# Mixture-of-experts pairs with the fuller expert first, and an arm for pairs of two small experts

## The chip, the cores and the metric

The kernel runs on one core of a Trainium2 chip. The core has five engines with queues of their own: TensorE (PE: matrix products, with a separate row for its weight loads), VectorE (DVE), ScalarE (ACT), GpSimd (POOL) and SyncE (SP), which here issues the loads. Sixteen DMA engines move data between the memory and the core's on-chip buffers. Products are summed in PSUM, a second on-chip memory, and copied out by ACT and DVE. The metric is the time of one execution on the device, in microseconds.

## The reference

Two transformer blocks of two layers each, over 256 tokens of width 1024, in float32. The change lies in the second block, in the mixture of experts that ends each of its two layers. A router picks two of sixteen experts for each token, and an expert is a SwiGLU network of inner width 512:

```python
for e in range(N_EXPERTS):
    he = jax.nn.silu(t @ w_gate[e]) * (t @ w_up[e])
    y = y + combine[:, e:e + 1] * (he @ w_down[e])
```

The router has four groups of four experts, takes the best group for a token, and in it the two best experts. With 256 tokens and two choices an expert has 32 tokens on average. On the inputs that are timed the reference's router gives these counts (expert p and expert p + 8, which the kernel treats as a pair):

| pair | 0 | 1 | 2 | 3 | 4 | 5 | 6 | 7 |
|---|---|---|---|---|---|---|---|---|
| layer 0 | 52, 29 | 24, 50 | 16, 20 | 50, 55 | 9, 48 | 29, 33 | 26, 18 | 32, 21 |
| layer 1 | 12, 79 | 12, 81 | 28, 72 | 22, 78 | 21, 17 | 25, 8 | 20, 14 | 14, 9 |

## The kernel before

All weights are read from memory once, over SP's queue. Most of the program multiplies dense matrices, split into a high and a low part. The expert stage is the function `moe(l, ...)`, called once a layer, and it works on plain float32.

**Pairs and slots.** Experts p and p + 8 share a pair of 128 slots. Each gets 64, or, where one has more than 64 tokens and the other at most 32, 96 and 32 (`ga`, L1757 and L1758). `slot` (L1774) says which slot a token has in a pair, and `onehot(p)` (L1780) makes a 0/1 matrix of it, tokens by slots. `gather` multiplies the normalized tokens with it into `xg_b` (L1828), `places` makes the slots' weights and the transposed matrix for the way back. Tokens that don't fit go to extra rounds behind the eight pairs; on these inputs there are none.

**One pair.** `pair()` computes the gate product (tile pg), the up product (pu), the activation, a transposition (tr), two halves of the down product (pd), and the way back to tokens (py). Gate and up have 8 steps over the width (KD), each half of down has 4. The slots are the stationary side and the weights the moving side, 512 columns wide. Every step issues one product for each strip of columns in `SEG` (L1848): two of 64, or four of 32; strips of different columns work side by side. One such product is two records in the profile.

**Branches.** Which strips a pair needs is known only after routing. `products()` (L1852) puts three arms into TensorE's program and picks one by a register that is read from `gi` (L1760; `reg`, L1931): 64 + 64 for value 2, 96 + 32 for 3, 32 + 96 otherwise. `reg(0)` stands ahead of the first gather in TensorE's queue.

**The ring of weights.** A pair has 12 pieces of 1 MiB: gate, up and down, each in two halves of the contracted width, each for two experts. `pieces()` (L1607) issues the loads in this order into a ring of 20 buffers (RING); a buffer is loaded again when the product that reads it is done. From piece 84 on (the last pair) each load is cut in two. Each load also waits for the load eight places ahead of it. The ring is full by the end of the router; only pair 0's gate frees the first buffers.

**Order.** The order of the engines' instructions follows the program's code, moved by a scheduler where nothing pins it; `pin()` holds the products of a pair in place. In a pair, the next pair's `gather` stands between the up product and the transposition, and again behind the transposition. In the last pair there is none, and the way back of the first half stands between the two parts of the second down half.

Of the kernel before, what the change touches and what calls it, by code (L numbers as in the profile page):

```python
# [7 lines left out]
F32 = mybir.dt.float32  # L8
F32R = mybir.dt.float32r
I32 = mybir.dt.int32  # L10
# [18 lines left out]
RING = 20  # L29
LNEXP = "natural_log_exp_and_others"  # L30
# [95 lines left out]
def build(tc, I, out, dump=None, upto=99):  # L126
    nc = tc.nc
    coff, ctot = _const_layout()
    with ExitStack() as ctx:
# [1456 lines left out]
        def moe(l, a, op, pre=None, post=None):  # L1586


            with ExitStack() as c1:
# [16 lines left out]

                def pieces(upto):  # L1607
# [138 lines left out]

                A2 = [128, 2, 8]
# [11 lines left out]
                gi = mp.tile([128, 8], I32, name="gi")  # L1759
                V.tensor_scalar(gi, ga[:, 0], 0.03125, None, op0=OP.mult)  # L1760
# [8 lines left out]
                V.tensor_scalar(sl[:, :, 0:8], pos[:, :, 0:8], 1.0, None, op0=OP.add)  # L1769
                V.scalar_tensor_tensor(sl[:, :, 8:16], pos[:, :, 8:16], 1.0, ga[:, 0:1, :].to_broadcast(A2),  # L1770
# [15 lines left out]
                ohs = {0: onehot(0)}  # L1786

# [64 lines left out]
                def products(p, x, n_k, w_, gr_, ks=None):  # L1852


                    def arm(n):
                        for k in ks or range(n_k):
                            ws, kp = w_(k)
                            for o, m, e in SEG[n]:
                                mm(p[o:o + m, :], x[:, k, o:o + m], ws[e][kp], start=k == 0, stop=k == n_k - 1,  # L1859
                                   skip_group_check=True)  # L1860
                    if gr_ is None:
                        arm(2)
                        return
                    with tc.issue_after(last[ENG.PE]):
                        with tc.If(gr_ == 2) as c:
                            arm(2)
                        with c.Else():
                            with tc.If(gr_ == 3) as c2:
                                arm(3)
                            with c2.Else():  # L1870
                                arm(1)

                def pair(pl, w_, gr_, nxt=lambda i: None, last_=False):

                    pg, pu = psum("pg"), psum("pu")
                    products(pg, xg_b, KD, lambda k: (w_("exp_w_gate_2", k // 4), k % 4), gr_)
                    products(pu, xg_b, KD, lambda k: (w_("exp_w_up_2", k // 4), k % 4), gr_)
                    act = tm()
                    S.activation(act, pg, AF.Silu)
                    V.tensor_mul(act, act, pu)  # L1880
# [4 lines left out]
                    for i in range(4):  # L1885
                        pin(PE.transpose(p[:, i * 128:(i + 1) * 128], act.rearrange("s (j k) -> s k j", k=4)[:, i], ident))
# [4 lines left out]
                    def down(dd, between=None):  # L1891
                        pd = psum("pd")
                        cs = slice(dd * 512, (dd + 1) * 512)
                        for ks in (range(0, 2), range(2, 4)) if between else (None,):
                            products(pd, hT, 4, lambda k: (w_("exp_w_down_2", k // 2), k % 2 * 2 + dd), gr_, ks)
# [34 lines left out]
                def reg(p):  # L1930
                    return nc.values_load(gi[0:1, p:p + 1], engines=[ENG.PE], min_val=1, max_val=3)  # L1931
# [5 lines left out]
                for p in range(8):  # L1937
# [15 lines left out]
                    pair(pl[p], lambda nm, hf: [wpiece[p, e, nm, hf] for e in range(2)], regs[p], nxt, p == 7)  # L1953
# [7 lines left out]
                with tc.For_i(0, n_extra, 1) as it:  # L1961
# [50 lines left out]
                    pair(places(oh2, w2_, 0), w_, None, last_=True)  # L2012
# [51 lines left out]
```

## Time and profile before

| | |
|---|---|
| median of three runs (lowest, highest) | 2056.05 us (2055.13, 2057.55) |
| the profiled execution, its own time | 2052.47 us |
| its span | 2050.7 us |
| TensorE busy, share of the span | 95% |
| weight loads of TensorE | 78% |
| DVE, ACT | 63%, 36% |
| read from memory over the span | 530.65 MB, 259 GB/s |
| expert stage of layer 0, first gate product to last product | 1411.8 to 1639.5 us |
| expert stage of layer 1, first gate product to end of span | 1807.5 to 2050.7 us |

The shares are means over stages with different limits. Positions are microseconds from the start of the span. A busy TensorE is not a TensorE at its peak, since products are pipelined; the granted clock (PEclk) stands beside it as a share of full speed.

### The profile page before, as it was taken

How to read it: one execution, taken by the hardware profiler on the slowest of the kernel's cores; microseconds unless marked ns; L12 is line 12 of the kernel's file. 1: busy time of each engine (PE TensorE's matmuls, PEld its weight loads, DVE VectorE, ACT ScalarE, POOL GpSimd, SP SyncE). 2: the span in 40 equal slices, each digit the busy share in tenths (PEclk: the TensorE clock that was granted, in tenths of full speed). 3: DMA queues.
4: the chain of work that ended last, by engine and by line, in shares of the span. 5: the costliest groups of instructions: out<-in, count | busy, mean ns of one | idle time of the engine just before them, and what ended most of it. 6: DMA issues, size and time to landing. Idle time of an engine off the chain costs nothing. (4 is left out here: it accounts for less than half of the span.)

```text
span 2050.7 us, 34453 instructions
## 1 busy us (share of the span) xinstructions
PE 1945.3 (95%) x14344; PEld 1599.1 (78%) x14344; DVE 1286.9 (63%) x2188; ACT 734.0 (36%) x1075; POOL 64.6 (3%) x60
## 2 busy tenths in 40 slices
PE   6999999999899999999999999998999889889997
PEld 5889899888699989999999999975444488744443
DVE  6357677858797959796798777853223287533222
ACT  4322222245454444445654445441000167500001
POOL 0000000011010010001010010000000010000000
PEclk8999999999999999999999999999999999989999
DMA  8678697734396869776486946468999544879992
GB/s 296 241 252 297 245 325 270 258 103 124 104 335 216 301 172 321 254 261 236 165 299 210 317 150 218 156 233 327 412 416 413 216 149 145 339 321 416 416 411 90
DMA packets 240525, 534.76 MB, mean 261 GB/s; under 512 B 13132, under 2 KB 168128, under 8 KB 206528
## 3 DMA queue, kind: packets, MB, share of 16 engines
q1 hardware_dynamic: 237424, 531.54, 72.0%
q8 instruction: 162, 2.65, 0.5%
q10 hardware_dynamic: 2896, 0.21, 0.2%
q14 instruction: 43, 0.35, 0.0%
HBM read 530.65 MB, written 1.07 MB: 259 GB/s over the span
## 5 line engine op out<-in xcount | busy, mean ns | idle before, releaser
L448 PE MATMUL pa<-hh,whl 128*128 128x258 f32 (+1 forms) x880 | 252.4, 287 | 3.6 <-ACT hh L516 3.6
L450 PE MATMUL pa<-hh,whl 128*128 128x258 f32 (+1 forms) x880 | 249.5, 283 | 4.9 <-DVE whl L419 4.9
L449 PE MATMUL pa<-hl,whl 128*128 128x258 f32 (+1 forms) x880 | 249.4, 283 | 3.3 <-DVE hl L517 3.3
L448 PE MATMUL pb<-hh,whl 128*128 128x258 f32 (+1 forms) x880 | 249.3, 283 | 0.8 <-ACT s L564 0.8
L449 PE MATMUL pb<-hl,whl 128*128 128x258 f32 (+1 forms) x880 | 249.0, 283 | 0.0
L450 PE MATMUL pb<-hh,whl 128*128 128x258 f32 (+1 forms) x880 | 248.9, 283 | 0.0
L324 DVE SCALAR_TENSOR_TENSOR macc<-modw,cst,macc 128x1024 f32<-128x1024 f32 (+1 forms) x182 | 219.9, 1235 | 23.0 <-DMA modw<-in_w_mod_dram 16.1
L418 ACT ACTIVATE whl<-w13r 128x2048 fp32r<-128x2048 f32 x88 | 168.5, 1914 | 179.7 <-PE pb L450 86.3
L419 DVE TENSOR_TENSOR whl<-w13r,whl 128x2048 fp32r<-128x2048 f32 x88 | 201.6, 2291 | 38.5 <-ACT whl L418 38.5
L450 PE MATMUL py<-gh,whl 128*128 128x256 f32 (+1 forms) x704 | 216.7, 308 | 2.7 <-DVE whl L419 2.7
L448 PE MATMUL py<-gh,whl 128*128 128x256 f32 (+1 forms) x704 | 218.4, 310 | 0.1
L449 PE MATMUL py<-gl,whl 128*128 128x256 f32 (+1 forms) x704 | 216.3, 307 | 0.0
L448 PE MATMUL lin<-hh,whl 128*128 128x258 f32 x640 | 188.6, 296 | 5.6 <-ACT hh L516 5.6
L449 PE MATMUL lin<-hl,whl 128*128 128x258 f32 x640 | 181.9, 285 | 3.3 <-DVE hl L517 3.3
L450 PE MATMUL lin<-hh,whl 128*128 128x258 f32 x640 | 181.4, 284 | 0.0
L448 PEld LDWEIGHTS pa<-hh,whl 128*128 128x128 f32 x880 | 166.8, 189 | 11.6 <-ACT hh L516 3.8
L450 PEld LDWEIGHTS pa<-hh,whl 128*128 128x128 f32 x880 | 167.3, 190 | 5.7 <-DVE whl L419 5.3
L449 PEld LDWEIGHTS pa<-hl,whl 128*128 128x128 f32 x880 | 167.7, 191 | 4.1 <-DVE hl L517 3.9
L448 PEld LDWEIGHTS pb<-hh,whl 128*128 128x128 f32 x880 | 166.8, 190 | 1.8 <-ACT s L564 1.0
L450 PEld LDWEIGHTS pb<-hh,whl 128*128 128x128 f32 x880 | 166.9, 190 | 0.4 <-issue 0.4
L449 PEld LDWEIGHTS pb<-hl,whl 128*128 128x128 f32 x880 | 166.9, 190 | 0.0
L418 ACT ACTIVATE whl<-w2r 128x768 fp32r<-128x768 f32 (+3 forms) x80 | 90.7, 1143 | 160.4 <-PE py L450 106.2
(444 smaller groups left out, 3766.7 us busy)
## 6 DMA issues: line engine op xcount, KB each, us to landing
w13r<-in_ffn_w_dram SPq DMA_DIRECT2D x86, 1024.0 KB
modw<-in_w_mod_dram SPq DMA_DIRECT2D x62, 1024.0 KB
ew<-in_exp_w_down_dram SPq DMA_DIRECT2D x54, 1024.0 KB
ew<-in_exp_w_gate_dram SPq DMA_DIRECT2D x54, 1024.0 KB
ew<-in_exp_w_up_dram SPq DMA_DIRECT2D x52, 1024.0 KB
modw<-in_ada_w_dram SPq DMA_DIRECT2D x48, 1024.0 KB
w2r<-in_ffn_w_dram SPq DMA_DIRECT2D x18, 1536.0 KB
w2r<-in_ffn_w_dram SPq DMA_DIRECT2D x12, 1280.0 KB
```

The source lines that it names most:

```text
L324: V.scalar_tensor_tensor(acc[h], x, c, acc[h], op0=OP.mult, op1=OP.add)
L418: S.activation(h, src, AF.Copy)
L419: V.tensor_sub(l, src, h.bitcast(F32))
L448: mm(p, ah, bh, start=start, stop=False)
L449: mm(p, ah, bl, start=False, stop=False)
L450: mm(p, al, bh, start=False, stop=stop)
```

## The change

For the first two pairs nothing changes but the layout of the activation in `pair()`. From the third pair on (SORTED = 2):

- The expert with more tokens comes first. `swp` says where the two change places, and the loads take the expert's number from a register on SP (`order(p)`), read from rows 1 and 2 of a larger `gi`.
- The branch has three other arms: both experts at most 32 tokens (`light`, value 4), 64 + 64 (value 2), and 96 + 32. In the new arm each expert has 32 slots, and these stand twice, in columns 0 to 63 and 64 to 127. One step multiplies four strips of 32: both experts with a piece of the first half of the contracted width and both with one of the second half. That takes half the steps and leaves two partial sums.
- The partial sums of the gate are added ahead of the activation (`oth`). Those of the up product are added by a product with the identity plus, in a light pair, a matrix that swaps halves (`summing`); it stands in the place of the transposition. Those of down are added by the way back, whose one-hot has the slots twice.
- The same instructions for `oth` and `summing` run in all pairs from the third on, with a factor of 0 where the pair isn't light.
- The router has more small steps on DVE, and `gi` is computed behind the first one-hot.

```diff
+                def order(p):
+                    if p not in orders:
+                        orders[p] = [nc.values_load(gi[0:1, 1 + i, p:p + 1], engines=[ENG.SP], min_val=0, max_val=15)
+                                     for i in range(2)]
+                    return orders[p]
...
-                                wpiece[todo[n + j]] = piece(bufs[(n + j) % RING], I[nm][l, p + 8 * e], nm, hf, ks)
+                                w = I[nm][l, p + 8 * e] if p < SORTED else \
+                                    I[nm][l][bass.ds(order(p)[e], 1)].rearrange("o a b -> (o a) b")
+                                wpiece[todo[n + j]] = piece(bufs[(n + j) % RING], w, nm, hf, ks)
...
-                gi = mp.tile([128, 8], I32, name="gi")
-                V.tensor_scalar(gi, ga[:, 0], 0.03125, None, op0=OP.mult)
+                V.tensor_mul(light, c32[:, 0], c32[:, 1])
+                V.memset(light[:, :SORTED], 0.0)
...
+                V.tensor_tensor(swp[:, SORTED:], swp[:, SORTED:], cnt[:, 1, SORTED:], op=OP.is_lt)
...
+                    V.scalar_tensor_tensor(gl[:, i], light, -32.0, ga[:, i], op0=OP.mult, op1=OP.add)
+                V.tensor_mul(st[:, 0], gl[:, 1], swp)
+                V.tensor_mul(st[:, 1], gl[:, 0], swp)
+                V.tensor_sub(st[:, 1], gl[:, 0], st[:, 1])
...
-                    V.tensor_tensor(oh, iota1[:, None, :].to_broadcast([128, 2, 128]),
-                                    slot[:, :, p:p + 1].to_broadcast([128, 2, 128]), op=OP.is_equal)
+                    V.tensor_tensor(oh[:, :, 0:64], iota1[:, None, 0:64].to_broadcast([128, 2, 64]),
+                                    slot[:, :, p:p + 1].to_broadcast([128, 2, 64]), op=OP.is_equal)
+                    V.scalar_tensor_tensor(oh[:, :, 64:128], iota1[:, None, 64:128].to_broadcast([128, 2, 64]),
+                                           l64[:, p:p + 1], slot[:, :, p:p + 1].to_broadcast([128, 2, 64]),
+                                           op0=OP.subtract, op1=OP.is_equal)
...
+                    def arm_light():
+                        for k in range(h) if ks is None else range(ks[0] // 2, ks[-1] // 2 + 1):
+                            for o in range(4):
+                                ws, kp = w_(k + o // 2 * h)
+                                mm(p[o * 32:o * 32 + 32, :], x[:, k + o // 2 * h, o * 32:o * 32 + 32], ws[o % 2][kp],
+                                   start=k == 0, stop=k == h - 1, skip_group_check=True)
...
+                    a, b, c_ = ((4, arm_light), (2, lambda: arm(2)), lambda: arm(3)) if srt else \
+                        ((2, lambda: arm(2)), (3, lambda: arm(3)), lambda: arm(1))
...
+                    V.scalar_tensor_tensor(x.rearrange("p (h j) -> p h j", h=2), i2[:, ::-1, :], light[:, p:p + 1], i2,
+                                           op0=OP.mult, op1=OP.add)
...
+                        S.activation(oth[0:64, :], pg[64:128, :], AF.Copy, scale=lt[64:128, :])
+                        V.tensor_scalar(oth[64:128, :], pg[0:64, :], lt[0:64, :], None, op0=OP.mult)
+                        V.tensor_add(oth, oth, pg)
+                        S.activation(kj, by_k(oth), AF.Silu)
...
-                        pin(PE.transpose(p[:, i * 128:(i + 1) * 128], act.rearrange("s (j k) -> s k j", k=4)[:, i], ident))
+                        o_ = p[:, i * 128:(i + 1) * 128]
+                        pin(PE.transpose(o_, kj[:, i], ident) if lt is None else mm(o_, kj[:, i], sm_, start=True, stop=True))
```

How instructions move, at three places. First DVE in the router of layer 0, before, from the register's source `gi` to the first one-hot `oh` (a row is a line of the kernel, an operation, what it writes and reads, and the shape):

```order
L1760 TENSOR_SCALAR gi<-ga 128x8
L1770 SCALAR_TENSOR_TENSOR sl<-pos,ga 128x2x8
L1766 TENSOR_TENSOR fit<-pos,ga 128x32
L1804 TENSOR_TENSOR left<-pos,ga 128x16
L1767 TENSOR_TENSOR fit<-fit,ch 128x32
L1805 TENSOR_TENSOR left<-left 128x8
L1772 TENSOR_TENSOR sl<-sl,fit 128x32
L1806 TENSOR_SCALAR left<-left 128x8
L1774 TENSOR_TENSOR slot<-sl 128x16
L1808 SCALAR_TENSOR_TENSOR left<-left 128x8
L1783 TENSOR_TENSOR oh<-c_iota_13207,slot 128x256
```

And the same place of the kernel after, from the first one-hot on:

```order
L1804 TENSOR_TENSOR slot<-sl 128x16
L1849 TENSOR_TENSOR left<-pos,ga 128x16
L1814 TENSOR_TENSOR oh<-c_iota_13207,slot 128x2x64
L1816 SCALAR_TENSOR_TENSOR oh<-c_iota_13207,l_15042,slot 128x2x64
L1827 TENSOR_TENSOR gf<-gf,l_15042 128x8
L1850 TENSOR_TENSOR left<-left 128x8
L1933 SCALAR_TENSOR_TENSOR w_14713<-c_ident,light 128x128
L1828 TENSOR_SCALAR gi<-gf 128x8
```

`gi` stood ten rows ahead of the one-hot; now it stands behind both halves of it, with three rows between, one of them a 128x128 matrix of `summing`.

Second, TensorE, the gate product of pair 3, before (the three arms, each closed by a jump; a row of products counts the instructions of one arm):

```order
L1865 COMPARE_AND_BRANCH
L1859 MATMUL pg<-ew,nx 64x512 x16
L1865 UNCONDITIONAL_BRANCH
L1868 COMPARE_AND_BRANCH
L1859 MATMUL pg<-ew,nx 32x512 x32
L1868 UNCONDITIONAL_BRANCH
L1859 MATMUL pg<-ew,nx 32x512 x32
L1868 UNCONDITIONAL_BRANCH
```

And after:

```order
L1921 COMPARE_AND_BRANCH
L1913 MATMUL pg<-ew,nx 32x512 x16
L1921 UNCONDITIONAL_BRANCH
L1924 COMPARE_AND_BRANCH
L1906 MATMUL pg<-ew,nx 64x512 x16
L1924 UNCONDITIONAL_BRANCH
L1906 MATMUL pg<-ew,nx 32x512 x32
L1924 UNCONDITIONAL_BRANCH
```

The first arm has 16 products of 32 columns; the 64 + 64 arm is now the second and is reached by a second comparison; the arm for 32 + 96 is gone.

Third, SP's queue where the loads of pair 2 begin, before:

```order
L1623 DMA ew<-in_exp_w_down_dram 128x2048 x2
L1623 DMA ew<-in_exp_w_gate_dram 128x2048 x2
L1865 UNCONDITIONAL_BRANCH x2
L1623 DMA ew<-in_exp_w_gate_dram 128x2048 x2
L1623 DMA ew<-in_exp_w_up_dram 128x2048 x2
```

And after:

```order
L1636 DMA ew<-in_exp_w_down_dram 128x2048 x2
L1614 TENSOR_LOAD gi
L1614 ISA x2
L1614 TENSOR_LOAD gi
L1614 ISA x2
L1636 ISA
L1636 DMA ew<-in_exp_w_gate_dram 128x2048
L1921 UNCONDITIONAL_BRANCH x2
L1636 ISA
L1636 DMA ew<-in_exp_w_gate_dram 128x2048
```

Two register loads from `gi` stand ahead of the pair's first load, and one register instruction ahead of each load; before, the same loads were issued back to back.

## Rows read from the trace of the kernel before

**Rows 1.** The page's second part: rate of all transfers in 40 equal slices.

```profile
GB/s 296 241 252 297 245 325 270 258 103 124 104 335 216 301 172 321 254 261 236 165 299 210 317 150 218 156 233 327 412 416 413 216 149 145 339 321 416 416 411 90
```

**Rows 2.** Table by windows, one stretch: stretch, us, engines, PEclk, DMA share, GB/s.

```profile
1441.00:1472.00 31.00, 31.00 (x172) 14.53 (x170) 9.81 (x22) 1.97 (x3) 0.00 (x0) 1.00 1.02 415
```

**Rows 3.** Groups by shape, 1380 to 2051: gate products, count, busy us, mean ns, idle.

```profile
L1859 PE MATMUL pg<-ew,nx 128*64 128x512 f32 x384 | 85.0, 595 | 0.0
...
L1859 PE MATMUL pg<-ew,nx 128*32 128x512 f32 x256 | 28.9, 593 | 1.0 <-issue 0.9
```

**Rows 4.** Timeline of TensorE, pair 2 of layer 0: start us, us, instruction, count.

```profile
1467.92 7.09 PE L1859 MATMUL pg<-ew,nx 128*64 128x512 f32 x32
1474.83 7.04 PE L1859 MATMUL pu<-ew,nx 128*64 128x512 f32 x32
...
1483.69 0.64 PE L1886 MATMUL tr<-c_ident,tm 128*128 128x128 f32 x4
...
1486.05 7.09 PE L1859 MATMUL pd<-ew,tm 128*64 128x512 f32 x32
...
1495.82 7.09 PE L1859 MATMUL pg<-ew,nx 128*64 128x512 f32 x32
```

**Rows 5.** Timeline of TensorE, layer 1, pairs 0, 1 and 3; in brackets the idle before.

```profile
1807.50 7.07 PE L1859 MATMUL pg<-ew,nx 128*32 128x512 f32 x64
...
1837.09 7.07 PE L1859 MATMUL pg<-ew,nx 128*32 128x512 f32 x63 [0.85 <-issue]
...
1903.95 7.05 PE L1859 MATMUL pu<-ew,nx 128*32 128x512 f32 x48 [2.27 <-issue]
```

**Rows 6.** Table by windows: start and end of the refills, and one clock.

```profile
1416.00:1418.00 2.00, 2.00 (x12) 0.69 (x10) 0.00 (x0) 0.00 (x0) 0.00 (x0) 1.00 0.75 184
...
1612.00:1614.00 2.00, 2.00 (x12) 0.63 (x10) 1.33 (x4) 0.00 (x0) 0.00 (x0) 1.00 0.54 210
1616.00:1618.00 2.00, 1.97 (x10) 0.43 (x6) 0.00 (x0) 0.00 (x0) 0.00 (x0) 1.00 0.22 69
...
1814.00:1816.00 2.00, 2.00 (x24) 0.72 (x20) 0.00 (x0) 0.60 (x1) 0.00 (x0) 1.00 0.74 217
...
2010.00:2012.00 2.00, 2.00 (x19) 2.00 (x18) 1.38 (x3) 0.59 (x1) 0.00 (x0) 1.00 0.16 64
...
1904.00:1906.00 2.00, 2.00 (x12) 0.54 (x16) 0.00 (x0) 0.00 (x0) 0.00 (x0) 0.53 1.01 418
```

**Rows 7.** Timeline of TensorE, the last pair of layer 0 and of layer 1.

```profile
1610.88 7.09 PE L1859 MATMUL pg<-ew,nx 128*64 128x512 f32 x32
...
1628.40 5.37 PE L1859 MATMUL pd<-ew,tm 128*64 128x512 f32 x24 [0.83 <-issue]
...
1638.41 1.10 PE L1906 MATMUL py<-dd 128*128 128x256 f32 x7 [0.40 <-DVE dd L1899]
...
2028.85 5.37 PE L1859 MATMUL pd<-ew,tm 128*64 128x512 f32 x24 [0.83 <-issue]
```

**Rows 8.** Timeline of all engines, router of layer 0.

```profile
1403.01 0.17 DVE L1749 TENSOR_SCALAR c<-pos 128x16 f32<-128x16 f32 x1 [0.80 <-PE pos L1743]
...
1403.89 0.16 DVE L1760 TENSOR_SCALAR gi<-ga 128x8 int32<-128x8 f32 x1
...
1404.92 0.42 DVE L1783 TENSOR_TENSOR oh<-c_iota,slot 128x256 f32<-128x256 f32 x1
...
1405.89 5.39 PE L1828 MATMUL ga<-oh,nx 128*128 128x128 f32 x32 [2.93 <-DVE w L1810]
```

**Rows 9.** Timeline of all engines, pair 2 of layer 0: the two evictions.

```profile
1489.80 0.69 ACT L1898 ACTIVATE dd<-pd,sw 128x512 fp32r<-128x512 f32 x1 [14.12 <-PE pd L1859]
1490.52 0.75 DVE L1899 SCALAR_TENSOR_TENSOR dd<-pd,sw,dd 128x512 fp32r<-128x512 f32 x1 [3.67 <-ACT dd L1898]
```

**Rows 10.** Timeline of SP's queue: one issue of a quarter of a piece.

```profile
1508.79 0.33 SPq L1620 DMA_DIRECT2D ew<-in_exp_w_down_dram  x1
```

More of the change, by code (lines that the diff above doesn't have):

```diff
@@ L29 @@
 RING = 20
+SORTED = 2
 LNEXP = "natural_log_exp_and_others"
@@ L1758, in moe @@
                 V.tensor_scalar(ga[:, 1], ga[:, 0], -1.0, 128.0, op0=OP.mult, op1=OP.add)
-                gi = mp.tile([128, 8], I32, name="gi")
-                V.tensor_scalar(gi, ga[:, 0], 0.03125, None, op0=OP.mult)
+                light = mp.tile([128, 8], F32, name="light")
+                V.tensor_mul(light, c32[:, 0], c32[:, 1])
+                V.memset(light[:, :SORTED], 0.0)
+                swp = mp.tile([128, 8], F32, name="swp")
+                V.memset(swp[:, :SORTED], 0.0)
+                V.tensor_copy(swp[:, SORTED:], cnt[:, 0, SORTED:])
+                V.tensor_tensor(swp[:, SORTED:], swp[:, SORTED:], cnt[:, 1, SORTED:], op=OP.is_lt)
+                gl = mp.tile(A2, F32, name="gl")
+                st = mp.tile(A2, F32, name="st0")
+                for i in range(2):
+                    V.scalar_tensor_tensor(gl[:, i], light, -32.0, ga[:, i], op0=OP.mult, op1=OP.add)
+                V.tensor_mul(st[:, 0], gl[:, 1], swp)
+                V.tensor_mul(st[:, 1], gl[:, 0], swp)
+                V.tensor_sub(st[:, 1], gl[:, 0], st[:, 1])
+                l64 = mp.tile([128, 8], F32, name="l64")
+                V.tensor_scalar(l64, light, 64.0, None, op0=OP.mult)
                 pos = mp.tile(E2, F32, name="pos")
@@ L1850, in moe, with products @@
                        1: ((0, 32, 0), (32, 32, 1), (64, 32, 1), (96, 32, 1))}
-                def products(p, x, n_k, w_, gr_, ks=None):
+                def products(p, x, n_k, w_, gr_, srt=False, ks=None):
+                    h = n_k // 2
                     def arm(n):
@@ L1863, in products @@
                         return
+                    a, b, c_ = ((4, arm_light), (2, lambda: arm(2)), lambda: arm(3)) if srt else \
+                        ((2, lambda: arm(2)), (3, lambda: arm(3)), lambda: arm(1))
                     with tc.issue_after(last[ENG.PE]):
-                        with tc.If(gr_ == 2) as c:
-                            arm(2)
+                        with tc.If(gr_ == a[0]) as c:
+                            a[1]()
                         with c.Else():
-                            with tc.If(gr_ == 3) as c2:
-                                arm(3)
+                            with tc.If(gr_ == b[0]) as c2:
+                                b[1]()
@@ L1870, in products, with summing @@
                             with c2.Else():
-                                arm(1)
-                def pair(pl, w_, gr_, nxt=lambda i: None, last_=False):
+                                c_()
+                def summing(p):
+                    x = (w0, w1)[p % 2]
+                    i2 = ident.rearrange("p (h j) -> p h j", h=2)
+                    V.scalar_tensor_tensor(x.rearrange("p (h j) -> p h j", h=2), i2[:, ::-1, :], light[:, p:p + 1], i2,
+                                           op0=OP.mult, op1=OP.add)
+                    return x
@@ L1875, in pair @@
+                def pair(pl, w_, gr_, lt, sm_, srt=False, nxt=lambda i: None, last_=False):
                     pg, pu = psum("pg"), psum("pu")
-                    products(pg, xg_b, KD, lambda k: (w_("exp_w_gate_2", k // 4), k % 4), gr_)
-                    products(pu, xg_b, KD, lambda k: (w_("exp_w_up_2", k // 4), k % 4), gr_)
                     act = tm()
-                    S.activation(act, pg, AF.Silu)
-                    V.tensor_mul(act, act, pu)
+                    kj = act.rearrange("s (k j) -> s k j", k=4)
+                    by_k = lambda x: x.rearrange("s (j k) -> s k j", k=4)
+                    products(pg, xg_b, KD, lambda k: (w_("exp_w_gate_2", k // 4), k % 4), gr_, srt)
+                    if lt is None:
+                        S.activation(kj, by_k(pg), AF.Silu)
+                    else:
+                        oth = tm()
+                        S.activation(oth[0:64, :], pg[64:128, :], AF.Copy, scale=lt[64:128, :])
+                        V.tensor_scalar(oth[64:128, :], pg[0:64, :], lt[0:64, :], None, op0=OP.mult)
+                        V.tensor_add(oth, oth, pg)
+                        S.activation(kj, by_k(oth), AF.Silu)
+                    products(pu, xg_b, KD, lambda k: (w_("exp_w_up_2", k // 4), k % 4), gr_, srt)
+                    V.tensor_mul(kj, kj, by_k(pu))
@@ L1952, in moe @@
                         ohs[p + 1] = onehot(p + 1)
-                    pair(pl[p], lambda nm, hf: [wpiece[p, e, nm, hf] for e in range(2)], regs[p], nxt, p == 7)
+                    pair(pl[p], lambda nm, hf: [wpiece[p, e, nm, hf] for e in range(2)], regs[p],
+                         *((light[:, p:p + 1], summing(p), True) if p >= SORTED else (None, ident, False)), nxt, p == 7)
                     pieces(12 * p + 12 + RING)
@@ L2011, in w_ @@
                         return got[nm, hf]
-                    pair(places(oh2, w2_, 0), w_, None, last_=True)
+                    pair(places(oh2, w2_, 0), w_, None, None, ident, last_=True)
         op = even(mods["a0"])
```

18 lines of the change are left out of this document (14 added, 4 removed).

## The prediction

> **What bounds the kernel now.** I read the slices of the span first: the rate row stands near 412 GB/s in two blocks of slices, 28 to 30 and 34 to 38 [rows 1]. These are the two expert stages; no other stretch stays at such a rate. A table by windows then shows what limits them: 415 GB/s with a DMA share of 1.02, so all sixteen DMA engines are full, and at the same time TensorE is busy for the whole 31 us [rows 2]. Two resources are nearly level, and the question is which of them ends last.
>
> The groups by shape say which arms ran. The gate product has 384 records on 64-column arms, 32 a pair, so 12 pairs; and 256 on 32-column arms, 64 a pair, so 4 pairs [rows 3]. That fits the counts in the section on the reference: no pair but the first four of layer 1 has a count over 64. By the same counts seven pairs from the third on have both experts at 32 tokens or fewer: pairs 2, 6, 7 of layer 0 and 4, 5, 6, 7 of layer 1. They are what I call light.
>
> The timeline of TensorE prices a pair: gate 7.09 us, up 7.04, down 7.09, and the next pair's gate 27.9 us after this one's [rows 4]. The memory needs 12 pieces of 1,048,576 bytes for it; at 415 GB/s a piece takes 2.53 us, a pair 30.3 us. TensorE is the faster of the two, and lives on the lead of 20 pieces in the ring. So I compare two lines. TensorE: pair 7 of layer 0 starts at 1610.9, its down product at 1628.4, and its last product ends at 1639.5 [rows 7]. Memory: the first refill moves at about 1416.8 in layer 0 and 1815 in layer 1; 76 pieces at 2.53 us are 192 us, so an even stream would end at 1608.8 and 2007 [rows 6]. Really the engines finish unevenly: at 1612 to 1614 the share is 0.54 (with a first megabyte for the next stage among it) and 0.22 at 1616 to 1618; in layer 1 0.16 at 2010 to 2012 [rows 6]. I take 1613 and 2010 for the landing of the last piece, with 1608.8 to 1617 and 2007 to 2012 as bounds. Today that is 15 to 19 us before the down product wants it: TensorE sets the end, by this margin and no more.
>
> **The change part by part.**
>
> *Light arms.* Four products of 32 columns side by side cost what two of 64 do: 64 records in 7.07 us [rows 5] against 32 in 7.09 [rows 4]. A light arm has 4 steps in place of 8 for gate and for up, and 4 in place of 8 for the two down halves together, so it halves 7.09 + 7.04 + 7.09: 10.6 us less per light pair, 74 us over seven. Most of this can't reach the end, because the last piece can't land sooner.
>
> *Does pair 7 then wait for memory?* Layer 0: two light pairs before it take 21.2 us off 1610.9; the transposition that becomes a product costs at most a second 0.64 us [rows 4] in each of five pairs, 3 us; the later start below adds 2. Pair 7 is then ready at about 1595, its down product some 10 us after it (3.5 + 3.5 + 3 for activation and transposition), at 1605. The last piece lands at 1613 + 2. TensorE waits some 10 us. In layer 1 three light pairs come before, and it waits longer. So in both layers the end becomes landing plus what is left to do.
>
> *What is left after landing.* Layer 0 needs 11.1 us from the start of down to the end of the last product [rows 7]. The light down takes 3.55 off. The eviction of the first down half, 0.69 on ACT and 0.75 on DVE [rows 9], stood behind 1.8 us of products and now stands behind 0.9, which gives 0.9 back: 8.5 us. Layer 1 has 2050.7 - 2028.85 = 21.9 us from there to the end of the span, so 19.2.
>
> *The clock after a wait.* After an idle of 2.27 us TensorE's granted clock was 0.53, close to the lower level of 1.2 GHz, and 48 records took 7.05 us, where three quarters of 7.07 are 5.3 [rows 5, 6]: 1.8 us lost. I add 1.8 in each layer for the restart in pair 7; bounds 0 (the clock stays up) and 3.5 (all that TensorE still has to do, some 6 us, at half rate for most of it).
>
> *Router.* Ahead of the first one-hot DVE has 28 short instructions where it had 20. Twenty took 1403.01 to 1404.92, 0.096 each [rows 8], so 0.8 us more. The branch register moves behind the one-hot: it is loaded on TensorE's queue ahead of the gather, and gi now comes at about 1406.6, against 1404.05. From gi to the gather it was 1.84 us [rows 8]. If that load is what the gather waited for, it starts at 1408.4, 2.5 us later; if the one-hot was, 0.8. I take 2. Behind the gather stand the first gate product and, through the ring, all refills, so it moves the landing too. The memory hides nothing of it: the ring is full there.
>
> *Gate eviction.* From pair 2 on it is four passes (ACT copy, DVE scale, DVE add, ACT activation) where it was one: 0.69 + 0.75 + 0.75 + 0.69 = 2.9 us by the nearest rows [rows 9]. The up product, 3.5 us in a light arm, hides it. Without that cover, the gather between up and transposition has another microsecond; I cost it at nothing, below 1 us a pair otherwise, and that again only ahead of a wait for memory.
>
> *Loads by register.* SP gets two register loads per pair from pair 2 on and one register instruction ahead of each load. No row shows a load with a register address. The nearest is a plain issue, 0.33 us [rows 10]; SP may take 2.53 us per piece before the stream notices, and up to eight loads are in flight. I take nothing; the other end is the rival below. It can't gain: the engines are full.
>
> *Branches.* A 64 + 64 pair from pair 2 on tests twice, as the 96 + 32 pairs of layer 1 do now, whose gate takes 7.07 us [rows 5]: nothing.
>
> **Sum.** Layer 0: 1613 + 2 + 8.5 + 1.8 = 1625.3 against 1639.5, 14.2 us less. Layer 1 (its span positions as they are now): 2010 + 2 + 19.2 + 1.8 = 2033 against 2050.7, 17.7 less. Together 32. The profiled execution took 2052.5 us, 1.8 more than its span, so 2020.6; the median shown is 3.6 us above that execution, so 2024. Best ends: 1608.8 + 0.8 + 8.5 and 2007 + 0.8 + 19.2, 45 us less, 2011. Worst: 1617 + 2.5 + 8.5 + 3.5 and 2012 + 2.5 + 19.2 + 3.5, 21.5 less, 2034.5.
>
> The Trainium skill (DMA: Bandwidth & Descriptors, Specifications) puts the fabric's ceiling at 435 GB/s and the memory's limit per core at about 358. By the first the 76 pieces would end 9 us sooner in each layer, an estimate of 50 us less; by the second 31 us later, which would leave no gain at all. The trace holds 415 for tens of microseconds, so neither is used above.
>
> **Rivals.**
>
> A. *TensorE keeps waiting for its own instructions.* Six times in these stages it stood still with nothing to wait for ("issue"), for 0.85 to 2.27 us, the shortest and the longest of the six [rows 5]. If each of the four groups of products in a light pair paid 1.75, as they jump over two other arms in half the time, a light pair would lose 7 of 10.6. Pair 7 of layer 0 would be at its down product at 1605 + 14 + 5 = 1624 and end at 1632.5 (7 less), layer 1 at 2028.9 - 31.8 - 7 + 5 = 1995, with 3 x 7 + 5 for the waits 2021, and end at 2040 (11 less): 2038. Against: layer 1's pairs jump now too, and show three of these waits in 16 groups. The Trainium skill (Runtime: NRT & Kernel Launch, Instruction fetch mechanics) says that a taken branch to a place outside the fetched window stalls the engine until it is fetched; by it A is the outcome, and the waits of this trace could be such fetches, though far from one per jump.
>
> B. *TensorE alone sets the time*: 74 less, minus 4 for the router and 6 for the products that replace transpositions, 64: 1992. For it speaks that TensorE is busy throughout [rows 2]; against it that the engines are full in the same row.
>
> C. *The light arms bring nothing*: not entered, or four streams that slow each other. Then only the router's 4 us are left, 2060. The counts and rows 5 speak against it.
>
> D, the other side. *Register addresses make the queue slower than the stream.* Layer 0 and 1 load 144 pieces so. Once SP and the address work take over 2.53 us a piece, each 0.1 us costs 14 us; at 2.75 the gain of 32 is gone, and at 3.0 it is 68 - 32 = 36 slower: 2092. For it: no row shows such a load. Against it: 0.33 us for an issue, a sevenfold reserve.
>
> **Chances.** The forecast 0.71 (2011 to 2035), A 0.13, B 0.05, C 0.04, D 0.07. The prediction is 2024. For 8 in 10 the range takes in half of A and the slack at the fast end: 2009 to 2040. What a measurement of this kernel can tell from no change is 0.2%, 4 us. Faster: forecast, A and B, 0.89. C lies on the border: 0.03 for no change, and 0.08 with D for slower.
>
> **What would show it.** In the profile after: pg groups with 16 steps' records in 3.5 us in seven pairs; waits of TensorE for a DMA of ew, about 10 us in pair 7 of each layer and next to none before; 415 GB/s unchanged; the last product of the expert stage near 1625; a clock near 0.5 just behind the wait; the first gather 2 us later. It is wrong if TensorE is late at pair 7 with "issue" ahead of its groups (A), if the rate falls under 400 in the steady part (D), or if the landing is not the last to come.

## The result, and the profile after

Beside each other on one chip, four runs of either kernel: before 2056.8 us (2055.13 to 2062.48), after 2024.66 us (2020.24 to 2029.16); ratio 0.9839, interval 0.9806 to 0.9872. The change takes 32 us off, and 2024 had been forecast. The profiled execution after took 2027.96 us with a span of 2026.2, one of the longer ones.

The first look goes to the rate in the slices of the page, as in [rows 1].

```profile
GB/s 295 233 252 305 236 320 282 285 76 156 46 349 201 345 134 336 220 328 186 205 233 280 251 216 239 106 208 291 384 415 416 398 139 167 264 276 388 418 415 260
```

Both blocks near 415 GB/s are still there: counted from 0, slices 28 to 31 hold 384 to 416 and slices 36 to 38 hold 388 to 418, and the last slice has 260 where it had 90. The rate has not risen: the same bytes fill the same engines, so what was saved lies elsewhere.

A light pair is the next thing to see: TensorE's timeline, pair 2 of layer 0 (start us, us, instruction, count, in brackets the idle before), against [rows 4].

```profile
1473.06 3.64 PE L1913 MATMUL pg<-ew,nx 128*32 128x512 f32 x32
1476.52 3.62 PE L1913 MATMUL pu<-ew,nx 128*32 128x512 f32 x32
1481.10 2.02 PE L1873 MATMUL ga<-oh,nx 128*128 128x128 f32 x16 [0.96 <-DVE tm L1955]
1482.96 1.06 PE L1962 MATMUL tr<-w,tm 128*128 128x128 f32 x8
...
1485.73 3.64 PE L1913 MATMUL pd<-ew,tm 128*32 128x512 f32 x32
...
1492.88 1.51 PE L1906 MATMUL pg<-ew,nx 128*64 128x512 f32 x6 [0.74 <-PE py L1982]
```

Gate, up and down take 3.6 us where they took 7.1; from this pair's gate to the next it is 19.8 us where it was 27.9. So 8.1 of the 10.6 us arrive. Two small prices stand in the brackets: 0.96 us ahead of the next pair's gather, which waits for the product with up (L1955), and 0.74 ahead of the next gate product.

Where the time goes then is told by pair 7. TensorE's timeline, layer 0, after, against [rows 7]:

```profile
1599.03 3.64 PE L1913 MATMUL pg<-ew,nx 128*32 128x512 f32 x32
1603.46 1.05 PE L1913 MATMUL pu<-ew,nx 128*32 128x512 f32 x4 [0.79 <-PE pg L1913]
1605.36 1.04 PE L1913 MATMUL pu<-ew,nx 128*32 128x512 f32 x2 [0.85 <-DMA ew<-in_exp_w_up_dram]
...
1609.17 1.90 PE L1913 MATMUL pu<-ew,nx 128*32 128x512 f32 x10 [0.22 <-DMA ew<-in_exp_w_up_dram]
...
1613.91 1.05 PE L1913 MATMUL pd<-ew,tm 128*32 128x512 f32 x4 [0.83 <-issue]
1616.03 5.75 PE L1913 MATMUL pd<-ew,tm 128*32 128x512 f32 x20 [1.07 <-DMA ew<-in_exp_w_down_dram]
...
1626.18 1.09 PE L1982 MATMUL py<-dd 128*128 128x256 f32 x7 [0.40 <-DVE dd L1975]
```

No product of pair 7 waited for a weight before; now up and down wait piece by piece. The group of 20 records looks like one slow stretch behind the wait that ends at 1616.03, but the waits go on inside it. They show in the row of TensorE's own weight loads, of which one stands ahead of each product:

```profile
1616.03 0.18 PEld L1913 LDWEIGHTS pd<-ew,tm 128*32 128x32 f32 x2 [1.98 <-DMA ew<-in_exp_w_down_dram]
1617.29 0.20 PEld L1913 LDWEIGHTS pd<-ew,tm 128*32 128x32 f32 x6 [1.07 <-DMA ew<-in_exp_w_down_dram]
1618.56 0.18 PEld L1913 LDWEIGHTS pd<-ew,tm 128*32 128x32 f32 x2 [1.08 <-SPq L2038]
1619.88 0.14 PEld L1913 LDWEIGHTS pd<-ew,tm 128*32 128x32 f32 x2 [1.14 <-SPq L2038]
```

They end 1.26 to 1.32 us apart, and half a piece, as the loads of the last pair are cut, takes 1.26 us at 415 GB/s. For the last two the profile names an issue on SP's queue; by the semaphores in the trace these two loads were complete at 1618.52 and 1619.84. So the last half piece of layer 0 is used at 1619.88. In layer 1 the last wait ends at 2008.50:

```profile
1994.25 1.34 PE L1913 MATMUL pu<-ew,nx 128*32 128x512 f32 x2 [2.17 <-DMA ew<-in_exp_w_up_dram]
...
2005.97 1.06 PE L1913 MATMUL pd<-ew,tm 128*32 128x512 f32 x6 [0.23 <-DMA ew<-in_exp_w_down_dram]
2007.23 1.05 PE L1913 MATMUL pd<-ew,tm 128*32 128x512 f32 x2 [0.20 <-DMA ew<-in_exp_w_down_dram]
2008.50 1.90 PE L1913 MATMUL pd<-ew,tm 128*32 128x512 f32 x10 [0.22 <-DMA ew<-in_exp_w_down_dram]
```

The table by windows (stretch, us, engines, granted clock, DMA share, GB/s), against [rows 2, 6]:

```profile
1420.00:1422.00 2.00, 2.00 (x12) 0.72 (x10) 0.00 (x0) 0.00 (x0) 0.00 (x0) 1.00 0.53 106
1502.00:1532.00 30.00, 30.00 (x170) 14.67 (x168) 10.15 (x22) 4.35 (x5) 0.00 (x0) 1.00 1.01 414
1612.00:1616.00 4.00, 2.13 (x12) 1.06 (x12) 0.69 (x1) 0.00 (x0) 0.00 (x0) 1.00 1.03 385
1616.00:1620.00 4.00, 3.97 (x11) 0.69 (x12) 0.00 (x0) 0.00 (x0) 0.00 (x0) 0.58 0.95 328
...
1930.00:1960.00 30.00, 23.86 (x190) 14.97 (x193) 11.87 (x25) 3.22 (x4) 0.00 (x0) 0.94 1.01 415
2006.00:2008.00 2.00, 1.80 (x8) 0.25 (x8) 0.00 (x0) 0.00 (x0) 0.00 (x0) 1.00 0.22 88
2008.00:2010.00 2.00, 1.78 (x11) 0.46 (x10) 0.00 (x0) 0.42 (x1) 0.00 (x0) 1.00 0.04 8
```

Late in layer 1 the DMA engines are full (1.01), while TensorE is busy 23.86 us of 30. None of the 6.14 us between is a wait for a weight: they are two issue waits of 2.65 and 3.49 us, in which TensorE waits for nothing that the profile shows. Before, such a pause would have moved the end; now the landing comes after it. That the two lines have changed places is shown by pair 7.

To add up, each layer is measured from the first router product (`pos`), so that what happened earlier drops out. The stage between is the second layer's work ahead of that product.

| stretch | before | after | difference | forecast |
|---|---|---|---|---|
| up to `pos` of layer 0 | 1401.7 | 1403.6 | +1.9 | 0 |
| layer 0, `pos` to last product | 237.8 | 223.7 | -14.1 | -14.2 |
| stage between | 157.5 | 161.4 | +3.9 | 0 |
| layer 1, `pos` to end of span | 253.6 | 237.5 | -16.1 | -17.7 |

The two expert stages give 30.2 us in this pair of profiles. The other two lines are stretches that the change doesn't touch, and the last section shows that they vary from kernel to kernel without it.

### The profile page after: what moved, and what is told of

It reads as the page before. It is cut to its first block, busy times and chain, and to the rows that moved or that the text cites. A ratio compares the mean times of both kernels' runs of the same rounds, so it can differ in the third digit from the quotient of the medians.

```text
span 2026.2 us, 35049 instructions
## 1 busy us (share of the span) xinstructions
PE 1903.2 (94%) x14392; PEld 1585.0 (78%) x14392; DVE 1312.7 (65%) x2276; ACT 749.2 (37%) x1087; POOL 64.3 (3%) x60
## 5 line engine op out<-in xcount | busy, mean ns | idle before, releaser
L326 DVE SCALAR_TENSOR_TENSOR macc<-modw,cst,macc 128x1024 f32<-128x1024 f32 (+1 forms) x182 | 219.8, 1235 | 21.7 <-DMA modw<-in_w_mod_dram 13.7
```

The source lines that it names most:

```text
L326: V.scalar_tensor_tensor(acc[h], x, c, acc[h], op0=OP.mult, op1=OP.add)
```

## The experiments

**1. No light arm.** What carries the gain?

```diff
-                V.memset(light[:, :SORTED], 0.0)
+                V.memset(light, 0.0)
```

> The changed kernel, but the vector that marks a pair as light is set to zero for all pairs: the light arm is never taken, everything else of the change (ordering, loads by register, the longer router, the gate eviction in four passes, products in place of transpositions) stays. Theory (the light arms let the landing of the last weight piece set the end): without them TensorE sets the end again, at the time of before plus about 2.4 us per layer for the router and up to 0.42 us for the products in place of transpositions in six pairs per layer, together some 5 to 10 us: 2058 to 2068 us. In the trace the last down product starts long after the last piece landed and waits for no DMA. Rival (the gain comes from somewhere else in the change, such as the order of the loads): near 2025.

Measured: 2057.69 us (2051.01 to 2061.51, ten runs) beside 2055.32; ratio 1.0013, interval 1.0003 to 1.0023. All that the change adds costs 2.4 us, a little less than expected, and without the light arms nothing is gained. TensorE sets the end again; its last down product in layer 0:

```profile
1627.05 5.37 PE L1906 MATMUL pd<-ew,tm 128*64 128x512 f32 x24 [0.83 <-issue]
```

By the windows of that trace the DMA share is 0.05 from 1616 to 1618: the down product starts some 10 us after the landing and waits for no transfer, as in [rows 7].

**2. Light arms in all pairs from the third on.** Does TensorE still set the end?

```diff
-                V.tensor_scalar(gi[:, 0], gf, 0.03125, None, op0=OP.mult)
+                V.tensor_scalar(gi[:, 0], gf, 0.0, 4.0, op0=OP.mult, op1=OP.add)
```

> The changed kernel with the branch register set to 4 for every pair: every pair from the third on takes the light arm (it leaves out part of the tokens of five pairs). TensorE then has five pairs' worth of 10.6 us less to do, 53 us; the bytes to load are the same. Theory (after the change the landing of the last piece sets the end): no further gain, 2020 to 2030, and long waits of TensorE for DMA instead. Rival 1 (TensorE still sets the end, by its work): 53 us less than the changed kernel, near 1972. Rival 2 (each light group pays for its jump with an issue wait): a part of that, 1985 to 2015, or no gain without waits for DMA.

Measured: 2021.82 us (2017.31 to 2027.75), ratio 0.9833 to before. Five more pairs shed their 10.6 us, 53 in all; 2.8 us arrive, which the spread of either kernel (10 and 9 us) does not tell from nothing. The groups by shape of this kernel (count, busy us, mean ns, idle and what ended it) show waits in their place, most of them for weights:

```profile
L1913 PE MATMUL pu<-ew,nx 128*32 128x512 f32 x384 | 62.8, 642 | 19.1 <-DMA ew<-in_exp_w_up_dram 11.9 <-issue 7.2
L1913 PE MATMUL pd<-ew,tm 128*32 128x512 f32 x384 | 55.9, 597 | 7.2 <-DMA ew<-in_exp_w_down_dram 5.0 <-issue 1.7 <-SPq L2038 0.5
L1913 PE MATMUL pg<-ew,nx 128*32 128x512 f32 x384 | 54.9, 625 | 5.4 <-DMA ew<-in_exp_w_gate_dram 5.4
```

After the change TensorE's work no longer sets the time.

**3 and 4. Half of the refills left out, in either kernel.** What would TensorE need alone? In the loop that issues the pieces, the same three lines in both:

```diff
                             for j, (p, e, nm, hf) in enumerate(todo[n:n + 1 + again]):
+                                if again and hf == 1:
+                                    wpiece[todo[n + j]] = rows4(bufs[(n + j) % RING])
+                                    continue
```

> The kernel before, but from the 21st weight piece of a layer on the second halves are not loaded (the products multiply with what lies in the buffers, so the second half of K is wrong): 38 of 76 pieces per layer less, TensorE's work unchanged. Theory (before, TensorE sets the end by 15 to 19 us): time as before, 2046 to 2057. Rival (memory sets the end already before): clearly less, 2030 or under.

> The changed kernel with the same pieces left out (second halves from the 21st piece on; the second half of K is computed with what lies in the buffers). Memory is far from the end now, so this is the time that TensorE alone needs. Theory (landing sets the end of the changed kernel): the full 74 us of seven light pairs less the router and the products in place of transpositions, so 58 to 66 us under the kernel before with the same omission, near 1990. Rival (waits of TensorE for its own instructions bind the changed kernel): 2010 or more, with issue waits of 1 to 3.5 us in many groups of the light pairs.

Measured: 2047.87 us (2046.65 to 2051.28) for before, ratio 0.9957; 1991.05 us (1990.49 to 1991.35) for after. Before, the loads left out were worth 7.5 us; after, 33.6. TensorE alone saves 56.8 us, where rival B put 64. Pair 7 of layer 0 without memory, TensorE's timeline of experiment 4:

```profile
1594.57 3.64 PE L1916 MATMUL pg<-ew,nx 128*32 128x512 f32 x32
1598.03 3.62 PE L1916 MATMUL pu<-ew,nx 128*32 128x512 f32 x32
1602.55 1.16 PE L1965 MATMUL tr<-w,tm 128*128 128x128 f32 x8 [0.91 <-DVE tm L1958]
1604.49 2.78 PE L1916 MATMUL pd<-ew,tm 128*32 128x512 f32 x24 [0.78 <-DVE tm L1966]
...
1611.70 1.09 PE L1985 MATMUL py<-dd 128*128 128x256 f32 x7 [0.41 <-DVE dd L1978]
```

From the gate's start to the last product's end 18.2 us, against 28.2 in the changed kernel (1599.03 to 1627.27): pair 7 loses 10.0 us to memory, as forecast. In layer 1 it is 30.2 against 19.8. Under the full stream TensorE also comes later to pair 7, 195.4 against 191.9 us after `pos` in layer 0 and 198.5 against 186.8 in layer 1; in layer 1 4.5 of these 11.7 us are issue waits (10.9 against 6.4), the rest was not taken apart. The brackets of the changed kernel hold only 2.4 and 3.1 us of DMA waits, since pieces that arrive one by one also stretch the groups between them. A wait is better read from the distance of two instructions than from its brackets.

**5. Constant addresses.** Do register addresses cost?

```diff
-                                w = I[nm][l, p + 8 * e] if p < SORTED else \
+                                w = I[nm][l, p + 8 * e] if p < 8 else \
```

> The changed kernel with constant addresses for the weight loads of all pairs, so no register is read on the queue that issues them (in the pairs whose two experts change places the products then meet the other expert's weights, which leaves the work and the bytes as they are but not the values). Theory (register addresses cost nothing, since the engines are full and the issue has a large reserve): as the changed kernel, within 4 us, 2020 to 2029, with the same 405 to 419 GB/s in the steady part. Rival (address work slows the queue): faster by 5 us or more, under 2018, and a higher rate.

Measured: 2023.8 us (2021.41 to 2027.44), beside 2023.69 (2022.49 to 2030.96) for the changed kernel, which was run once more as the neighbour of experiments 5 to 7:

> The changed kernel unchanged, as the neighbour of the others on the same chip: 2020 to 2029 us.

The two steady windows of experiment 5:

```profile
1502.00:1532.00 30.00, 30.00 (x168) 14.67 (x166) 9.95 (x21) 4.35 (x5) 0.00 (x0) 1.00 1.02 415
1930.00:1960.00 30.00, 25.07 (x204) 14.24 (x200) 13.06 (x29) 4.47 (x6) 0.00 (x0) 0.94 1.01 414
```

414 and 415 GB/s with either kind of address: they cost nothing. Rival D falls.

**6. The first gate half earlier.** If the landing ends everything, an earlier start of the stream should end it earlier. Not shown below: this kernel also has the early register number of experiment 7, and the up product of pair 0 stands in the same arm as the second gate half.

```diff
+                    if pl is None:
+                        products(pg, xg_b, KD, gw, gr_, srt, range(0, 4))
+                        gather(ohs[0], 4)
+                        pl = places(ohs[0], wt[:, :, 0], 0)
+                        products(pg, xg_b, KD, gw, gr_, srt, range(4, 8), (pu, uw))
...
-                gather(ohs[0], 4)
-                pl = {0: places(ohs[0], wt[:, :, 0], 0)}
+                pl = {0: None}
```

> The changed kernel, computing the same, with one thing moved: in pair 0 of each layer the first half of the gate product (k 0 to 3) runs right behind the first gather, ahead of the second gather and the places, and the branch register of pairs 0 and 1 comes from a number of its own that DVE has early. So the first ring buffers come free earlier and the refills start earlier. Theory (the landing of the last piece sets the end of the changed kernel): the first refill moves some 3 to 6 us earlier in each layer, the landing and the end with it, 6 to 11 us less than the changed kernel beside it, 2012 to 2019. Rival 1 (TensorE or something behind the landing sets the end): no gain, within 3 us of it. Rival 2 (the stream ends at the same time since the engines' finish, not the start, decides): first refill earlier, landing not.

Measured: 2026.41 us (2024.98 to 2027.24), 2.7 more than its neighbour and 7.1 more than experiment 7, which has the early register alone: a miss. TensorE's timeline, layer 0:

```profile
1412.16 6.07 PE L1908 MATMUL pg<-ew,nx 128*64 128x512 f32 x16 [0.79 <-DVE nx L1877]
...
1422.08 3.65 PE L1908 MATMUL pg<-ew,nx 128*64 128x512 f32 x16 [1.25 <-DVE nx L1877]
```

and the windows there:

```profile
1412.00:1416.00 4.00, 3.84 (x10) 1.24 (x12) 0.11 (x1) 0.00 (x0) 0.00 (x0) 0.50 0.02 4
...
1418.00:1420.00 2.00, 2.00 (x18) 1.84 (x17) 0.00 (x0) 0.00 (x0) 0.00 (x0) 1.00 0.46 74
1420.00:1424.00 4.00, 2.75 (x18) 1.36 (x19) 1.55 (x5) 0.00 (x0) 0.00 (x0) 1.00 0.95 389
1424.00:1430.00 6.00, 6.00 (x32) 2.01 (x28) 0.00 (x0) 0.60 (x1) 0.00 (x0) 1.00 0.68 240
```

The first half ran at a granted clock of 0.50, behind TensorE's waits in the router, so it took 6.07 us where the later one took 3.65. The stream then got its first buffers, but not the next ones: the second half and up come later than in the changed kernel, and from 1424 to 1430 the rate is 240. The last weight load that waits comes 219.6 us after `pos` in layer 0 and 220.0 in layer 1, against 216.3 and 219.8 in the changed kernel. So the landing did not come earlier, and the end not either: an earlier start of the stream is worth nothing when the buffers behind it come late.

**7. Only the branch register earlier.** Pairs 0 and 1 get a register number of their own, which DVE has early; all else stays.

```diff
+                g0 = mp.tile([128, 8], I32, name="g0")
+                V.tensor_scalar(g0, ga[:, 0], 0.03125, None, op0=OP.mult)
...
-                    return nc.values_load(gi[0:1, 0, p:p + 1], engines=[ENG.PE], min_val=1, max_val=4)
+                    return nc.values_load(g0[0:1, p:p + 1] if p < SORTED else gi[0:1, 0, p:p + 1], engines=[ENG.PE],
+                                          min_val=1, max_val=4)
```

> The changed kernel, computing the same, with only the branch register of pairs 0 and 1 made from a number of its own that DVE has early; the order of the gate product stays. If the first gather of each layer waits for that register, as its 1.04 us behind the register's number suggests, it starts about 1 to 1.5 us earlier, and by the landing the end too: 2 to 3 us less than the changed kernel beside it, at the border of what can be measured. If the gather waits for the one-hot, the gather stays where it is and so does the time.

> The version with the early branch register once more, to tell its few us from the changed kernel's spread: its first five runs had a median of 2019.3 us, eight runs of the changed kernel lie between 2020.2 and 2031.0. If the earlier gather carries through the landing to the end (2 us earlier per layer at the first gate product), 2017 to 2022 again; if the first five were chance, 2023 to 2026.

Measured: 2019.27 us (2014.4 to 2024.35), ratio 0.9827, interval 0.9807 to 0.9847; the second time 2019.03 us (2017.01 to 2023.31), ratio 0.9818, interval 0.9799 to 0.9837. Its ten runs have a mean of 2019.5, the eight of the changed kernel 2024.9; the difference of 5.5 is three times its standard error of 1.7 (from the spread of both groups, which were not all run side by side). This version is faster than both kernels. The changed kernel's router first, all engines, layer 0:

```profile
1407.39 0.35 DVE L1816 SCALAR_TENSOR_TENSOR oh<-c_iota,l,slot 128x128 f32<-128x128 f32 x1
1408.08 0.17 DVE L1828 TENSOR_SCALAR gi<-gf 128x8 int32<-128x8 f32 x1
1409.29 6.34 PE L1873 MATMUL ga<-oh,nx 128*128 128x128 f32 x32 [4.45 <-DVE w L1855]
```

and TensorE of experiment 7, where `pos` began at 1399.58:

```profile
1403.98 5.29 PE L1875 MATMUL ga<-oh,nx 128*128 128x128 f32 x32 [3.17 <-DVE left L1852]
...
1409.81 1.51 PE L1908 MATMUL pg<-ew,nx 128*64 128x512 f32 x6
```

From `pos` to the gather it is 5.69 us in the changed kernel and 4.40 here (4.16 before), to the first gate product 12.6 and 10.2 (10.1 before). So the gather waited for the register, 1.04 us behind the number's end, and not for the one-hot, which ends 0.51 us ahead of the number; the bracket names another instruction of DVE, since the register load is no busy time. Another 1.05 us lie in the gather itself, 6.34 against 5.29: behind the longer wait its granted clock was 0.50 from 1409 to 1414, here 0.69 from 1404 to 1409. Layer 0 falls from 223.3 in the neighbour to 221.4 (221.6 the second time), layer 1 from 237.5 to 233.7 (235.6). In the first of the two profiles the last weight load that waits comes just as much earlier, 1.9 and 3.8 us.

**8. Four pieces fewer per layer.** A small dose, to see whether the end follows the bytes.

```diff
+                                if p == 4 and hf == 1 and nm != "exp_w_down_2":
+                                    wpiece[todo[n + j]] = rows4(bufs[(n + j) % RING])
+                                    continue
```

> The changed kernel, but four weight pieces of each layer are not loaded (the second halves of gate and up of both experts in pair 4, which is computed with what lies in the buffers). Theory (the landing of the last piece sets the end of the changed kernel): 4 x 2.53 us less per layer, 20 us in all, from 2024 to about 2004; TensorE alone would allow 1991, so nothing else stops it before that. Rival (part of the end is TensorE's own, and what the memory gives back is met by its work or its waits for instructions): 8 to 14 us less, 2010 to 2016.

Measured: 2015.55 us (2009.5 to 2021.7), ratio 0.9789: about 9 less, with a standard error of 3, not 20; the rival's range was met. Here the theory was too simple. The profiled execution is the longest of the four, 2021.7. In its layer 0 (218.7, 5 less) no product of pair 7 waits for a transfer any more, but TensorE gets there 197.7 us after `pos`, no sooner than in the changed kernel (195.4), and its down product takes 4.48 us at a granted clock of 0.57 where experiment 4 has 2.78: what TensorE needs under the full stream lies only some 5 us below the landing's line. In layer 1 the stream itself pauses; the windows of experiment 8:

```profile
1880.00:1890.00 10.00, 10.00 (x94) 4.59 (x89) 3.83 (x10) 1.38 (x2) 0.00 (x0) 1.00 0.73 279
1890.00:1900.00 10.00, 10.00 (x100) 3.06 (x96) 3.09 (x8) 2.16 (x2) 0.00 (x0) 1.00 0.59 223
```

TensorE is busy without a gap there, in the pairs with counts over 64; the DMA engines stand idle for 6.8 us there, of 10 saved, and SP's waits between 1870 and 1905 all end with products of TensorE, which free the buffers of the ring. The two lines are coupled by the ring, and a saving on one is worth only their distance at that point.

## Why the prediction was right, step by step

- *Two resources nearly level, TensorE last by 15 to 19 us.* Right in the order: experiments 1 and 3 leave the time nearly as it was, experiment 4 shows 33.6 us of memory behind the new end. The margin was smaller: by the semaphores in the trace of before the last pieces landed at 1615.05 and 2011.90, not 1613 and 2010, 13 and 17 us ahead of the down product. Of slices 34 to 38 in [rows 1] only 36 to 38 stand near 412, 34 and 35 hold 339 and 321; no sum uses them.
- *A light pair saves 10.6 us.* Mis-sized: 8.1 in pair 2 of layer 0, and 9.9 without the second halves in experiment 4, where that pair takes 18.0 us; in layer 1 pairs 4, 5 and 6 take 18.1, 26.6 and 22.1 us from gate to gate, 9.8, 2.9 and 8.0 less than before. Pair 5 holds the issue waits of 2.65 and 3.49 us. TensorE alone gains 56.8 us, 7 less than B's 64. For the forecast it hardly mattered, since TensorE waits at pair 7 anyhow.
- *The gate eviction costs nothing.* Not quite. The four passes run from 1476.85 to 1480.30, 3.45 us where 2.9 was summed, and end 0.16 us behind the up product:

```profile
1476.85 0.68 ACT L1950 ACTIVATE tm<-pg,light 64x512 f32<-64x512 f32 x1 [5.66 <-PE pg L1913]
1479.13 1.17 ACT L1953 ACTIVATE tm<-tm 128x512 f32<-128x512 f32 x1 [1.59 <-DVE tm L1952]
```

  These are ACT's two; the second took 1.17, not 0.69. The product with up follows at 1480.35, and the gather waits 0.96 us for it: under the 1 us that was named as the price without cover, and ahead of a wait for memory, as said.
- *TensorE waits some 10 us in pair 7, longer in layer 1.* Right by distances for the size: 10.0 and 10.4. In layer 1 it is hardly longer, since TensorE came to pair 7 later than its work alone asked for (experiment 4).
- *Landing 2 us later.* Mis-sized in both layers. The last half piece is used 216.3 us after `pos` in layer 0, forecast 213.3 (1613 + 2 - 1401.73), and 219.8 in layer 1, forecast 214.9. About 2 us of each difference lie in where the landing before was put (above); from there it moved by 2.9 and 4.9 us. The first gate product came 2.5 and 2.3 us later, and in layer 1 the stream itself ran slower for a while:

```profile
1850.00:1860.00 10.00, 10.00 (x92) 5.75 (x96) 3.42 (x5) 0.69 (x1) 0.00 (x0) 1.00 0.97 379
1860.00:1870.00 10.00, 10.00 (x94) 4.75 (x90) 4.74 (x13) 0.69 (x1) 0.00 (x0) 1.00 0.93 363
```

  With the windows beside them it ran at 363 to 406 GB/s from 1830 to 1880, which is worth 3.1 us against 415, behind a pair 1 that took 33.5 us with a TensorE stall of 2.13. The forecast let the stream run at one rate; that TensorE still paces it through the ring fits this, and experiment 8.
- *What is left, 8.5 and 19.2, and the clock, 1.8.* Together 10.3 and 21.0 forecast, 7.4 and 17.7 measured from the last wait on. The whole down product and what follows it take 8.3 us in experiment 4, near the 8.5 summed; but 14 of the 24 records ahead of the first eviction were done when the last half piece landed. The clock cost nothing at the end. In layer 0 it fell to 0.58 behind the wait, and the 20 records took 5.75 us where 24 took 2.78 in experiment 4, but their pace was the landings', 1.26 to 1.32 us apart; in layer 1 the waits lie as far apart at a granted clock of 1.00. In the seven profiles in which pair 7 waits for weights in both layers (after and experiments 2, 5, 6 and 7, the neighbour and the repetition among them) the remainder is 7.39 to 7.40 us in layer 0 and 17.67 to 17.81 in layer 1. So the end follows the landing in each of them.
- *Router +2.* The first gate product is 2.5 and 2.3 us later; the register was the main cause, by experiment 7.
- *Register loads 0, second branch test 0.* The first is shown by experiment 5. For the second, pairs of 64 + 64 now take 28.3 us, 0.4 more than before, with the product in place of the transposition in it (1.06 us against 0.64 in [rows 4]).
- *Rival A* has its place, but not at the end. TensorE's issue waits add up to 10.9 us in layer 1 up to pair 7, 6.5 before the change; they lie ahead of the landing. The count in the prediction was off: the trace before has five of these waits of 0.85 to 2.27 us, two of them in the 16 groups named, and two of 0.83 ahead of the last down products. The Trainium skill (Runtime: NRT & Kernel Launch, Instruction fetch mechanics) has a taken branch out of the fetched window stall its engine. The trace agrees in part: there are waits of up to 3.49 us, though in only a few of the 28 groups of the light pairs, and no run shows that they are such fetches.

That 2024 met 2024.66 is partly luck. In layer 0 a landing 3.0 us later than forecast met a remainder 2.9 shorter, in layer 1 it was 4.9 and 3.3. The mechanism held, and the range did not need this.

The total also came out nearer than the profiles alone would show. Between the two profiled executions lie 24.5 us; the one before ran 4.3 under the median beside it, the one after 3.3 over, which gives the 32.1 between the medians. The two expert stages hold 30.2 of them, 1.7 less than the forecast's 31.9.

## What to carry to other kernels

When two resources run nearly level, a saving on the later one counts only down to the point where the other ends, with the work that must follow it; work that out from where each would finish, and expect the rest to come back as waits. Look for these waits in the row of TensorE's weight loads as well: in the row of products, strips that still run can hide a wait, and a group held up by landings looks like one at a slow clock. A buffer ring couples the two, so look also at whether the stream pauses for buffers before you give it a rate. When an operation is moved behind others on a queue, check first whether a register or a flag that something waits for moves with it: that was some 5 us here for one small instruction.

## What was not expected of the hardware

TensorE's issue waits up to pair 7 are shorter in sum when the weight stream is halved: none in layer 0 in experiments 3 and 4, where before has 1.8 us and after 1.3; in layer 1 4.4 in experiment 3 against 6.5 in before, and 6.4 in experiment 4 against 10.9 in after. That would fit instructions that come over the same busy engines, but it is not shown: after, its neighbour and experiments 5, 6 and 7 have 7.5 to 12.0 in layer 1 under the full stream, and experiment 1, without light arms, has 2.8.

The stage between, which nobody touched, took 157.5 to 163.1 us in the twelve profiles. The part that differs most are the products from one wait of 1.14 us on to the next router product: 6.7 us in before and in experiment 6, 10.65 in the profile after, which is the whole difference of that line in the table. The windows of that stretch, after:

```profile
1752.00:1762.00 10.00, 9.87 (x47) 8.96 (x48) 2.93 (x10) 2.50 (x4) 0.00 (x0) 0.53 0.64 240
```

and before:

```profile
1764.00:1771.00 7.00, 5.88 (x48) 5.24 (x48) 3.60 (x11) 3.43 (x7) 0.00 (x0) 1.00 0.59 197
```

The same 48 instructions run at a granted clock near the lower level of 1.2 GHz in one and at 2.4 GHz in the other, after the same waits ahead of them. Experiment 6 holds the change and has the short form, so it doesn't belong to the change; why the clock is lower in some profiles stays open.
